# Two levels of a causal 4-token tree merged into one block, in the third branch of a hybrid decoder layer

## The chip, the cores and the metric

The kernel runs on one core of one Trainium2 chip. The metric is the device time of one launch in microseconds (us). Before the change it is 2781.73 us, the median of three runs (2780.98 to 2782.83).

## The reference

One decoder layer on 2048 tokens of width 1024, with 16 meta tokens in front. The normalised input goes through one projection, then through three causal mixers of four heads of 128, and gates and an output projection join them. The change touches only the third mixer, a gated linear recurrence (HGRN2). For one head, with queries `q`, keys `k`, values `v` and forget factors `f` per channel:

```
G = cumsum(log f) over the chunk
dec[i, j, d] = exp(G[i, d] - G[j, d])   for j <= i, else 0
a[i, j] = sum_d q[i, d] * k[j, d] * dec[i, j, d]
o = (q * exp(G)) @ state + a @ v
state = state * exp(G_end) + (k * exp(G_end - G))^T @ v
```

The entry `a[i, j]` between a key token j and a later token i needs the product of all factors `f` of the tokens j+1 to i, channel by channel, so it is no plain matrix product.

## The kernel before, in words

The sequence is worked through in four segments (`j`, 512 tokens each, `TQ`), and a segment in `NT` = 4 tiles of 128 tokens. Channels lie on the 128 partitions, tokens along the free dimension. `dense_work` (L1322) yields the projections and output products; each fp32 product is three matmuls with split operands (`mm3`, L167 to L169). At the bottom of the program every mixer's scan is woven into that stream by `weave` (L1392): each `yield` of a scan names an amount of time, and for it a share of dense matmuls is recorded. A scheduler of the tile framework then fixes each engine's order by its own estimate of times. The scans of heads 0 and 1 run side by side (`both`, L1284), then those of heads 2 and 3; so there are eight pairs, two in each segment.

`hg_scan` (L1103) computes `a` without exponentials of differences. It goes through seven levels, `s` = 1, 2, 4, ... 64. At level `s` the tokens are split into blocks of 2s; the pairs to be filled are those with j in the left and i in the right half. Two running tables are kept: `pf` holds, for a token, the product of the factors from the start of its block of `s` up to it, and `sf` the product from after it to the end of its block. The left halves of `kql` become `k * sf` (L1130; at level 1 a copy on GpSimd, L1128), the right halves `q * pf` (L1126). Then TensorE multiplies `kql` with itself, and only the entries of this level count. For s up to 16 that is sixteen 32x32 matmuls into one PSUM tile `z` (L1162), four tiles by four groups of 32 tokens; the text calls them one block. VectorE takes the level's entries out of `z` with a predicated copy (L1166) under the mask `lvl[:, lv]`, into the tile `AD`, which goes to the diagonal of `at` at level 16. For s = 32 and 64 the products at L1148 and L1136 fill `at` directly. L1178 and L1179 bring `sf` and `pf` to the next level; at level 1 two GpSimd instructions set `sf` (L1175, L1176). After the last level `at`, the values and the state `Sh` are multiplied (L1196 to L1199).

GpSimd also multiplies q by k for the diagonal (L1106), and `put_ob` (L398 to L402) has it subtract the high part of finished heads (`ob`, by the helper at L118). A sum over channels turns that product to tokens on TensorE (L380) and reduces it on VectorE (L367). The masks come from `c_lvl` through `load_levels` (L1465), once.

Of the kernel before, what the change touches and what calls it, by code (L numbers as in the profile page):

```python
# [15 lines left out]
P = 128  # L16
# [3 lines left out]
META = 16  # L20
TQ = 512
NQ = SEQ // TQ
NT = TQ // P
# [16 lines left out]
def kernel(  # L40
# [21 lines left out]
    nc = tc.nc  # L62
# [12 lines left out]
    def nm(s):  # L75
        uid[0] += 1
        return f"{s}_{uid[0]}"
# [5 lines left out]
    def slot(tag, shape=(P, WQ), dt=F32, bufs=None):  # L83
        return pool.tile(list(shape), dt, tag=tag, name=nm(tag), bufs=bufs or BUFS[tag])
# [10 lines left out]
    def p_z():  # L95
        return ps_z.tile([P, 512], F32, tag="z", name=nm("z"))
# [1006 lines left out]
    def hg_scan(j, h, st):  # L1103
        pf, kk, qq, vt, gate = st.pop(h)
# [4 lines left out]

        sf = slot("S")  # L1110
        at, ad = AT[h % 2], AD[h % 2]
        s = 1
        lv = 0
        while s < P:
            def v4(t):
                r_ = t[:, META:].rearrange("p (b two s) -> p b two s", two=2, s=s)
                return r_[:, :, 0], r_[:, :, 1]

            nb = TQ // (2 * s)
            kql = slot("S")  # L1120
            kl_, kr_ = v4(kql)
            pl_, pr_ = v4(pf)
            fl_, fr_ = v4(sf)
            kkl, _ = v4(kk)
            _, qqr = v4(qq)
            nc.vector.tensor_mul(kr_, qqr, pr_)  # L1126
            if s == 1:
                nc.gpsimd.tensor_copy(kl_, kkl)  # L1128
            else:
                nc.vector.tensor_mul(kl_, kkl, fl_)  # L1130
            z = p_z()
            if s == 64:

                for n in range(NT):
                    c, o = META + n * P, 64 * (n % 2)
                    nc.tensor.matmul(  # L1136
                        z[o : o + 64, n // 2 * 64 : n // 2 * 64 + 64], kql[:, c : c + 64], kql[:, c + 64 : c + P],
                        start=True, stop=True,
                    )
                for g in range(2):  # L1140
                    nc.scalar.copy(
                        at[:64, g::2, 64:], z[64 * g : 64 * g + 64, :P].rearrange("p (n c) -> p n c", n=2)
                    )
            elif s == 32:
                for n in range(NT):
                    for b in (0, 64):
                        c, o = META + n * P + b, b + 32 * (n % 2)
                        nc.tensor.matmul(  # L1148
                            z[o : o + 32, n // 2 * 32 : n // 2 * 32 + 32], kql[:, c : c + 32],
                            kql[:, c + 32 : c + 64], start=True, stop=True,  # L1150
                        )
                for b in (0, 64):
                    for g in range(2):
                        nc.scalar.copy(
                            at[b : b + 32, g::2, b + 32 : b + 64],
                            z[b + 32 * g : b + 32 * g + 32, :64].rearrange("p (n c) -> p n c", n=2),
                        )
            else:
                for n in range(NT):
                    for b in range(4):  # L1160
                        c = META + n * P + 32 * b
                        nc.tensor.matmul(  # L1162
                            z[32 * b : 32 * b + 32, n * 32 : (n + 1) * 32], kql[:, c : c + 32], kql[:, c : c + 32],
                            start=True, stop=True,
                        )
                nc.vector.copy_predicated(  # L1166
                    ad, lvl[:, lv : lv + 1].broadcast_to([P, NT, 32]),
                    z[:, :P].rearrange("p (n c) -> p n c", n=NT),
                )
                if s == 16:  # L1170
                    for b in range(4):
                        sl = slice(32 * b, 32 * b + 32)
                        nc.scalar.copy(at[sl, :, sl], ad[sl])
            if s == 1:
                nc.gpsimd.tensor_copy(fl_, pr_)  # L1175
                nc.gpsimd.memset(fr_, 1.0)  # L1176
            else:
                nc.vector.tensor_mul(fl_, fl_, pr_[:, :, s - 1 : s].broadcast_to([P, nb, s]))  # L1178
            nc.vector.tensor_mul(pr_, pr_, pl_[:, :, s - 1 : s].broadcast_to([P, nb, s]))  # L1179
            s *= 2  # L1180
            lv += 1
            yield 2.5
# [139 lines left out]
    def dense_work():  # L1322

        xs = norm_x0()
        for j in range(nq):
            y, yh, yl = [None] * KC, [None] * KC, [None] * KC
            pool_share[0] = 5
            for h in range(H):
                yield from sb_proj(j, xs, h, sst)
                if j == 0 and h == 0:  # L1330
                    load_levels()
# [76 lines left out]
    with tc.issue_after(marks["act"]), tc.issue_after(marks["dve"]), tc.issue_after(marks["pool"]):  # L1408
# [54 lines left out]
        lvl = const.tile([P, 5, 32], mybir.dt.uint8, name="lvl")  # L1463

        def load_levels():  # L1465
            lv32 = slot("D", (P, 5, 32))
            for b in range(4):
                sl = slice(32 * b, 32 * b + 32)
                nc.sync.dma_start(lv32[sl], c_lvl[sl, :5, sl])
            nc.vector.tensor_copy(lvl, lv32)  # L1470

    for j in range(nq):
# [104 lines left out]
```

## Time and profile before

| | |
|---|---|
| median of three runs | 2781.73 us |
| the profiled execution, its own time | 2781.62 us |
| its span, first to last instruction | 2779.8 us |
| TensorE busy | 2734.3 us, 98% |
| VectorE busy | 1469.8 us, 53% |
| ScalarE busy | 962.5 us, 35% |
| GpSimd busy | 744.0 us, 27% |
| mean granted TensorE clock | 0.997 |

The profiled execution lies 0.1 us below the median and 1.8 us above its span. Busy time of TensorE counts pipelined matmuls whose modelled ends overlap, so the price of a matmul is read from the starts in the timeline, not from its duration. A row of the timeline gives the start, the time, engine, line, operation and count; a note in brackets is the engine's idle time before it and what ended that.

### The profile page before, as it was taken

What the parts mean: (1) busy time and instruction counts of PE and PEld (TensorE: products, weight loads), DVE (VectorE), ACT (ScalarE), POOL (GpSimd) and SP (SyncE); (2) the same over time, 40 slices, a digit from 0 to 9 for tenths busy, and PEclk for the clock granted to TensorE, in tenths of its full rate; (3) what the DMA queues carried; (4) which work ended last, traced back from release to release, by engine and by line L of the source; (5) the groups of instructions that cost most, each with busy time, mean ns of one, the idle gap of its engine ahead of it and who ended that gap; (6) DMA issues with size and microseconds to landing.
All of it is one profiled execution on the core that took longest, in us unless ns stands there. A gap on an engine that the chain in (4) does not pass through costs nothing. (4 is left out here: it accounts for less than half of the span.)

```text
span 2779.8 us, 46064 instructions
## 1 busy us (share of the span) xinstructions
PE 2734.3 (98%) x17616; PEld 2258.6 (81%) x17616; DVE 1469.8 (53%) x2890; ACT 962.5 (35%) x2255; POOL 744.0 (27%) x1011
## 2 busy tenths in 40 slices
PE   7999999999999999999999999999999999999999
PEld 6898788888887888778888888877888877888887
DVE  5467637744357545543255775554325577556521
ACT  5454343343345212222144641222224455313120
POOL 4555214433132302112022240111212232302111
PEclk9999999999999999999999999999999999999999
DMA  7667746679554654547755456344764443554556
GB/s 259 227 205 255 264 164 217 237 255 322 188 169 148 194 175 129 159 152 245 231 176 175 145 168 189 115 151 148 250 209 148 157 160 121 170 157 122 160 159 211
DMA packets 200064, 520.51 MB, mean 187 GB/s; under 512 B 43104, under 2 KB 44064, under 8 KB 199844
## 3 DMA queue, kind: packets, MB, share of 16 engines
q1 hardware_dynamic: 199556, 517.50, 57.2%
q8 instruction: 139, 2.28, 0.3%
q14 instruction: 81, 0.66, 0.1%
q10 hardware_dynamic: 288, 0.07, 0.0%
HBM read 397.18 MB, written 120.31 MB: 186 GB/s over the span
## 5 line engine op out<-in xcount | busy, mean ns | idle before, releaser
L167 PE MATMUL acc<-xh,w 128*128 128x512 f32 (+2 forms) x2248 | 860.0, 383 | 4.5 <-DVE D L454 1.2
L168 PE MATMUL acc<-xl,w 128*128 128x512 f32 (+2 forms) x2248 | 847.3, 377 | 0.3 <-DVE xl L260 0.2
L169 PE MATMUL acc<-xh,w 128*128 128x512 f32 (+2 forms) x2248 | 845.1, 376 | 1.7 <-DVE w L118 1.7
L167 PEld LDWEIGHTS acc<-xh,w 128*128 128x128 f32 x2248 | 425.1, 189 | 80.4 <-DVE D L454 2.1
L169 PEld LDWEIGHTS acc<-xh,w 128*128 128x128 f32 x2248 | 425.1, 189 | 74.8 <-DVE w L118 2.2
L168 PEld LDWEIGHTS acc<-xl,w 128*128 128x128 f32 x2248 | 424.8, 189 | 69.7 <-DVE xl L260 1.3
L528 DVE TENSOR_TENSOR_SCAN S<-S,zero 128x128 f32<-128x128 f32 (+4 forms) x216 | 197.3, 917 | 143.1 <-ACT S L522 124.6
L118 POOL TENSOR_TENSOR w<-wraw,w 128x512 fp32r<-128x512 f32 x106 | 149.5, 1412 | 282.7 <-ACT w L147 246.9
L534 POOL TENSOR_TENSOR S<-S,S 128x256 f32<-128x256 f32 (+2 forms) x108 | 94.2, 873 | 396.4 <-DVE S L528 262.5
L522 ACT ACTIVATE S<-z,rq 128x128 f32<-128x128 f32 (+4 forms) x216 | 116.5, 539 | 132.4 <-PE z L169 85.2
L147 ACT CAST w<-wraw 128x512 fp32r<-128x512 f32 x182 | 112.3, 618 | 130.4 <-PE acc L169 59.2
L118 DVE TENSOR_TENSOR S<-tr,S 128x512 fp32r<-128x512 f32 (+4 forms) x176 | 104.9, 606 | 47.9 <-ACT S L562 47.4
L730 DVE SCALAR_TENSOR_TENSOR D<-D,cw,D 128x512 f32<-128x512 f32 (+1 forms) x144 | 120.2, 835 | 17.2 <-ACT D L728 15.0
L167 PE MATMUL acc<-ob,w 128*128 128x512 f32 x312 | 125.8, 405 | 1.4 <-ACT ob L401 1.4
L168 PE MATMUL acc<-ob,w 128*128 128x512 f32 x312 | 124.4, 399 | 0.0
L169 PE MATMUL acc<-ob,w 128*128 128x512 f32 x312 | 123.3, 396 | 0.0
L167 PE MATMUL av<-xh,w 128*128 128x512 f32 (+2 forms) x304 | 119.7, 394 | 0.7 <-ACT D L1059 0.7
L168 PE MATMUL av<-xl,w 128*128 128x512 f32 (+2 forms) x304 | 118.1, 389 | 0.0
L169 PE MATMUL av<-xh,w 128*128 128x512 f32 (+2 forms) x304 | 117.5, 386 | 0.0
L523 ACT ACTIVATE S<-z,rq 128x128 f32<-128x128 f32 (+4 forms) x216 | 116.0, 537 | 0.0
L562 ACT CAST S<-tr 128x512 fp32r<-128x512 f32 (+4 forms) x176 | 90.8, 529 | 64.4 <-PE tr L558 64.2
L1246 POOL TENSOR_TENSOR y<-y,g 128x512 f32<-128x512 f32 x32 | 46.8, 1461 | 236.3 <-DVE g L1244 236.3
(389 smaller groups left out, 4916.7 us busy)
## 6 DMA issues: line engine op xcount, KB each, us to landing
w<-wk SPq DMA_DIRECT2D x555, 512.0 KB, 3.5
wk<-w SPq DMA_DIRECT2D x184, 512.0 KB, 3.5
wraw<-in_w_in_dram SPq DMA_DIRECT2D x142, 256.0 KB, 3.8
D<-in_xq_dram SPq DMA_DIRECT2D x56, 256.0 KB, 4.3
S<-rows SPq DMA_DIRECT2D x48, 256.0 KB, 4.9
S<-dv SPq DMA_DIRECT2D x48, 256.0 KB, 4.3
out_dram<-D SPq DMA_DIRECT2D x32, 256.0 KB, 4.6
S<-dk SPq DMA_DIRECT2D x24, 264.0 KB, 3.0
```

Source lines behind the costliest of these rows:

```text
L118: (eng or nc.gpsimd).tensor_sub(out_, a, hi.bitcast(F32))
L147: nc.scalar.copy(hi, raw)
L167: nc.tensor.matmul(dst, lh, rh, start=first, stop=False)
L168: nc.tensor.matmul(dst, lh, rl, start=False, stop=False)
L169: nc.tensor.matmul(dst, ll, rh, start=False, stop=last)
L522: nc.scalar.activation(pc[:, :n], z[:, :n], AF.Sigmoid, scale=rq[:, NT + i : NT + i + 1])
L523: nc.scalar.activation(at[:, :n], z[:, :n], AF.Sigmoid, scale=rq[:, i : i + 1])
L528: nc.vector.tensor_tensor_scan(pc[:, 0:n][:, ::-1], pc[:, 0:n][:, ::-1], zero1.broadcast_to([P, n]), 1.0 if carry[i] is None else pc[:, n ...
L534: eng.tensor_mul(at[:, :n], at[:, :n], pc[:, 1 : n + 1])
L562: nc.scalar.copy(ath[:kw, cs_], tr[:kw, cs_])
L730: nc.vector.scalar_tensor_tensor(dst[:, c0:], raw[:, c0 + i : c0 + i + n], cw[:, ci, i : i + 1], dst[:, c0:], ALU.mult, ALU.add)
L1246: nc.gpsimd.tensor_add(y[e], y[e], g)
```

## The change

The levels s = 1 and s = 2 become one step on blocks of four tokens (0 to 3). Two tiles, `lh` and `rh`, take the place of `kql`: `lh` holds k0 f1, k1, k2 f3, k3, and `rh` holds, at the places 0 to 3, q3, q1, q2 f2, q3 f2 f3. One block of sixteen matmuls `lh` by `rh` then holds the entries of the pairs 0-1, 0-2, 1-2, 0-3 and 1-3 at their own places. The pair 2-3 needs another right side than the pairs 0-3 and 1-3; it stands in the column of token 0, which no pair uses, and a second predicated copy moves that column to the place of token 3. The mask of the first copy is level 2's with the level-1 column of token 1 joined to it, once, in `load_levels`. Two GpSimd copies fill the plain parts of `lh` and `rh`; four VectorE products fill the rest. After the copies `sf` and `pf` are brought to level 4 by four products, a GpSimd copy and a memset. The two yields of 2.5 become one of 5.0, and the loop starts at s = 4.

```diff
-        s = 1
-        lv = 0
+        def blocks(z, lh, rh):
+            for n in range(NT):
+                for b in range(4):
+                    c = META + n * P + 32 * b
+                    nc.tensor.matmul(
+                        z[32 * b : 32 * b + 32, n * 32 : (n + 1) * 32], lh[:, c : c + 32], rh[:, c : c + 32],
+                        start=True, stop=True,
+                    )
+            return z[:, :P].rearrange("p (n c) -> p n c", n=NT)
+        def quad(t):
+            return t[:, META:].rearrange("p (b i) -> p b i", i=4)
+        fq, kq, qq4, sq_ = quad(pf), quad(kk), quad(qq), quad(sf)
+        lh, rh = slot("S"), slot("S")
+        lq, rq = quad(lh), quad(rh)
+        mul = nc.vector.tensor_mul
+        nc.gpsimd.tensor_copy(lq[:, :, 1::2], kq[:, :, 1::2])
+        nc.gpsimd.tensor_copy(rq[:, :, 0:2], qq4[:, :, 1::2][:, :, ::-1])
+        mul(sq_[:, :, 1], fq[:, :, 2], fq[:, :, 3])
+        mul(lq[:, :, 0::2], kq[:, :, 0::2], fq[:, :, 1::2])
+        mul(rq[:, :, 2], qq4[:, :, 2], fq[:, :, 2])
+        mul(rq[:, :, 3], qq4[:, :, 3], sq_[:, :, 1])
+        zv = blocks(p_z(), lh, rh)
+        nc.vector.copy_predicated(ad, lvl[:, 1:2].broadcast_to([P, NT, 32]), zv)
+        nc.vector.copy_predicated(
+            ad[:, :, 3::4], lvl[:, 0:1, 3::4].broadcast_to([P, NT, 8]), zv[:, :, 0::4]
+        )
+        mul(sq_[:, :, 0], fq[:, :, 1], sq_[:, :, 1])
+        nc.gpsimd.tensor_copy(sq_[:, :, 2], fq[:, :, 3])
+        nc.gpsimd.memset(sq_[:, :, 3], 1.0)
+        mul(fq[:, :, 1], fq[:, :, 0], fq[:, :, 1])
+        mul(fq[:, :, 3], fq[:, :, 1], sq_[:, :, 1])
+        mul(fq[:, :, 2], fq[:, :, 1], fq[:, :, 2])
+        yield 5.0
+        s = 4
+        lv = 2
...
             nc.vector.tensor_mul(kr_, qqr, pr_)
-            if s == 1:
-                nc.gpsimd.tensor_copy(kl_, kkl)
-            else:
-                nc.vector.tensor_mul(kl_, kkl, fl_)
+            nc.vector.tensor_mul(kl_, kkl, fl_)
...
-            if s == 1:
-                nc.gpsimd.tensor_copy(fl_, pr_)
-                nc.gpsimd.memset(fr_, 1.0)
-            else:
-                nc.vector.tensor_mul(fl_, fl_, pr_[:, :, s - 1 : s].broadcast_to([P, nb, s]))
+            nc.vector.tensor_mul(fl_, fl_, pr_[:, :, s - 1 : s].broadcast_to([P, nb, s]))
...
+            nc.vector.tensor_copy(lv32[:, 1, 1::4], lv32[:, 0, 1::4])
             nc.vector.tensor_copy(lvl, lv32)
```

In the changed program the matmuls of all blocks stand at L1118, the two new predicated copies at L1140 and L1141, that of the later levels at L1198, the right and left products of the loop at L1167 and L1168, the tables' at L1203 and L1204, the level of 32 at L1186.

The scheduler sets the order anew, so rows move beyond the lines of the diff. On TensorE, the second pair of heads of the second segment, before (`acc` dense products, `tr` a turn to tokens, `z` a block):

```order
L380 MATMUL tr_12989<-ident,S_12986 128x128 x4
L1162 MATMUL z_12999<-S_12996 32x32 x16
L167 MATMUL acc_12976<-xh_7675,w_2535_12972 128x512
L168 MATMUL acc_12976<-xl_7676,w_2535_12972 128x512
L169 MATMUL acc_12976<-xh_7675,w_2535_12972 128x512
L167 MATMUL acc_12976<-xh_7723,w_2535_12972 128x512
L168 MATMUL acc_12976<-xl_7724,w_2535_12972 128x512
L169 MATMUL acc_12976<-xh_7723,w_2535_12972 128x512
L1162 MATMUL z_13029<-S_13026 32x32 x16
```

and now, from the same turn to tokens on:

```order
L380 MATMUL tr_12921<-ident,S_12918 128x128 x4
L1118 MATMUL z_12936<-S_12929,S_12928 32x32 x16
L167 MATMUL acc_12902<-xh_7860,w_2531_12900 128x512
L168 MATMUL acc_12902<-xl_7861,w_2531_12900 128x512
L169 MATMUL acc_12902<-xh_7860,w_2531_12900 128x512
L167 MATMUL acc_12902<-xh_7908,w_2531_12900 128x512
L168 MATMUL acc_12902<-xl_7909,w_2531_12900 128x512
L169 MATMUL acc_12902<-xh_7908,w_2531_12900 128x512
L167 MATMUL acc_12902<-xh_7956,w_2531_12900 128x512
L168 MATMUL acc_12902<-xl_7957,w_2531_12900 128x512
L169 MATMUL acc_12902<-xh_7956,w_2531_12900 128x512
L167 MATMUL acc_12971<-ob_11674,w_2516_12806 128x512
```

Blocks stood alone between dense matmuls, and still do; two of them are gone from the pair, and where the next one stood six dense matmuls later dense work goes on. TensorE's order, counted over all four segments, has 1024 block matmuls in 66 runs where it had 1280 in 77.

On VectorE, the start of the first pair of the third segment, before (`D_17769` and `D_18488` are the tables `pf` of the two heads):

```order
L398 TENSOR_TENSOR S_18461<-tr_18456,D_17713 128x512
L1126 TENSOR_TENSOR S_18635<-D_17828,D_17769 128x256
L1126 TENSOR_TENSOR S_18688<-D_18523,D_18488 128x256
L1179 TENSOR_TENSOR D_17769<-D_17769 128x256
L1126 TENSOR_TENSOR S_18721<-D_17828,D_17769 128x128x2
L1130 TENSOR_TENSOR S_18721<-D_17770,S_18634 128x128x2
```

and now (`D_17658` and `D_18377` are those tables):

```order
L398 TENSOR_TENSOR S_18350<-tr_18345,D_17602 128x512
L1136 TENSOR_TENSOR S_18524<-D_17659,D_17658 128x256
L1135 TENSOR_TENSOR S_18523<-D_17658 128x128
L1137 TENSOR_TENSOR S_18525<-D_17717,D_17658 128x128
L1136 TENSOR_TENSOR S_18595<-D_18378,D_18377 128x256
L1137 TENSOR_TENSOR S_18596<-D_18412,D_18377 128x128
L1135 TENSOR_TENSOR S_18594<-D_18377 128x128
L1138 TENSOR_TENSOR S_18525<-D_17717,S_18523 128x128
```

The first block of a pair hung on VectorE's first product; the first block of four hangs on the seventh (L1138 into `S_18525`).

On TensorE, later in the same pair, before (levels 8 and 16 of one head and 16 of the other, then level 32):

```order
L169 MATMUL acc_19069<-xh_14195,w_3719_19067 128x512
L167 MATMUL acc_19069<-xh_14233,w_3719_19067 128x512
L1162 MATMUL z_18888<-S_18885 32x32 x16
L1162 MATMUL z_18922<-S_18919 32x32 x16
L1162 MATMUL z_18957<-S_18954 32x32 x16
L1148 MATMUL z_18997<-S_18994 32x32 x8
L168 MATMUL acc_19069<-xl_14234,w_3719_19067 128x512
```

and now the same blocks:

```order
L169 MATMUL acc_18930<-xh_14008,w_3708_18926 128x512
L1118 MATMUL z_18749<-S_18746 32x32 x16
L1118 MATMUL z_18783<-S_18780 32x32 x16
L1118 MATMUL z_18818<-S_18815 32x32 x16
L167 MATMUL acc_18930<-xh_14046,w_3709_18928 128x512
L168 MATMUL acc_18930<-xl_14047,w_3709_18928 128x512
L169 MATMUL acc_18930<-xh_14046,w_3709_18928 128x512
L167 MATMUL acc_18930<-xh_14084,w_3709_18928 128x512
L1186 MATMUL z_18858<-S_18855 32x32 x8
```

The run of three blocks now stands earlier in the dense product, behind its fourth part of eight and not inside its seventh, and four dense matmuls have come between it and the matmuls of level 32. From the start of the pair to the run's third block there are 72 dense matmuls of 512 columns where there were 79. SP's order of DMAs is unchanged.

## Rows read from the trace of the kernel before

**Rows 1.** The page, busy time of the engines (us, share of span, instructions).

```profile
PE 2734.3 (98%) x17616; PEld 2258.6 (81%) x17616; DVE 1469.8 (53%) x2890; ACT 962.5 (35%) x2255; POOL 744.0 (27%) x1011
```

**Rows 2.** Waits of TensorE in the third branch: us in total, times, longest.

```profile
PE z L1148 <- DVE S L1126: 1.4, 2, 0.8
PE z L1162 <- DVE S L1126: 1.0, 1, 1.0
```

**Rows 3.** Groups by line, the blocks: busy us, mean ns of one, idle before.

```profile
L1162 PE MATMUL z<-S 128*32 128x32 f32 x2560 | 37.1, 199 | 1.0 <-DVE S L1126 1.0
```

**Rows 4.** Timeline of TensorE, one block alone: start us, us.

```profile
1103.90 0.39 PE L168 MATMUL acc<-xl,w 128*128 128x512 f32 x1
1104.13 0.40 PE L169 MATMUL acc<-xh,w 128*128 128x512 f32 x1
1104.46 0.46 PE L1162 MATMUL z<-S 128*32 128x32 f32 x32
1104.85 0.50 PE L168 MATMUL acc<-ob,w 128*128 128x512 f32 x1
1105.19 0.39 PE L169 MATMUL acc<-ob,w 128*128 128x512 f32 x1
```

**Rows 5.** Timeline of TensorE, a run of 6 records and one of 128.

```profile
437.88 0.40 PE L167 MATMUL acc<-ob,w 128*128 128x512 f32 x1
438.21 0.26 PE L1162 MATMUL z<-S 128*32 128x32 f32 x6
438.40 0.50 PE L168 MATMUL acc<-ob,w 128*128 128x512 f32 x1
438.74 0.39 PE L169 MATMUL acc<-ob,w 128*128 128x512 f32 x1
...
2539.70 0.40 PE L169 MATMUL av<-ob,w 128*128 128x512 f32 x1
2540.03 1.45 PE L1162 MATMUL z<-S 128*32 128x32 f32 x128
2541.41 0.50 PE L168 MATMUL acc<-ob,w 128*128 128x512 f32 x1
2541.74 0.39 PE L169 MATMUL acc<-ob,w 128*128 128x512 f32 x1
```

**Rows 6.** VectorE: one line's ns (min/median/max), and groups by form (busy us, mean ns).

```profile
L1126 DVE TENSOR_TENSOR S<-D,D x112: 408/420/1559, 427.9 to 2624.6; 128x256 f32<-128x256 f32 x112
...
L1166 DVE COPY_PREDICATED AD<-lvl,z 128x128 f32<-128x128 uint8 x80 | 23.5, 296 | 41.8 <-PE z L1162 41.8
L1003 DVE TENSOR_TENSOR r<-D,z 128x128 f32<-128x128 f32 x32 | 9.1, 284 | 17.9 <-PE z L1000 17.7
L534 DVE TENSOR_TENSOR S<-S,S 128x128 f32<-128x128 f32 x16 | 7.1, 443 | 1.9
```

**Rows 7.** Timeline of VectorE, first pair of the third segment.

```profile
1793.48 0.94 DVE L1126 TENSOR_TENSOR S<-D,D 128x256 f32<-128x256 f32 x2
1794.34 1.52 DVE L1179 TENSOR_TENSOR D<-D 128x256 f32<-128x256 f32 x1
...
1796.99 1.49 DVE L1178 TENSOR_TENSOR S<-S,D 128x256 f32<-128x256 f32 x1
1798.52 1.39 DVE L1179 TENSOR_TENSOR D<-D 128x256 f32<-128x256 f32 x1
...
1814.53 0.41 DVE L1130 TENSOR_TENSOR S<-D,S 128x256 f32<-128x256 f32 x1
1814.87 0.41 DVE L1179 TENSOR_TENSOR D<-D 128x256 f32<-128x256 f32 x1
```

**Rows 8.** Timeline of GpSimd, same pair.

```profile
1796.91 4.16 POOL L118 TENSOR_TENSOR ob<-S,ob 128x512 fp32r<-128x512 f32 x3
```

**Rows 9.** Timeline of TensorE, same pair.

```profile
1798.76 0.46 PE L1162 MATMUL z<-S 128*32 128x32 f32 x32
...
1815.76 0.46 PE L1162 MATMUL z<-S 128*32 128x32 f32 x32 [1.02 <-DVE S L1126]
1816.77 0.33 PE L1148 MATMUL z<-S 128*32 128x32 f32 x16 [0.55 <-DVE S L1126]
...
1817.42 0.63 PE L169 MATMUL acc<-xh,w 128*128 128x512 f32 x1
1817.84 0.63 PE L167 MATMUL acc<-xh,w 128*128 128x512 f32 x1
...
1820.79 0.39 PE L168 MATMUL av<-xl,w 128*128 128x512 f32 x1
```

**Rows 10.** One microsecond of that stretch: busy us by engine, granted clock, DMA share, GB/s.

```profile
1818.00:1819.00 1.00, 1.00 (x4) 0.81 (x3) 1.00 (x5) 0.01 (x1) 0.00 (x0) 0.50 0.00 0
```

**Rows 11.** Timeline of TensorE, a wait in the last segment's attention.

```profile
2307.00 0.50 PE L558 MATMUL tr<-ident,S 128*16 128x128 f32 x3 [1.41 <-POOL S L534]
```

**Rows 12.** Second pair of the third segment: an early product (VectorE) and the first block (TensorE).

```profile
1869.53 1.52 DVE L1126 TENSOR_TENSOR S<-D,D 128x256 f32<-128x256 f32 x1
...
1888.22 0.46 PE L1162 MATMUL z<-S 128*32 128x32 f32 x32
```

More of the change, by code (lines that the diff above doesn't have):

```diff
@@ L1158, in hg_scan @@
             else:
[L1159 to L1169, printed above, removed]
+                zv = blocks(z, kql, kql)
+                nc.vector.copy_predicated(ad, lvl[:, lv : lv + 1].broadcast_to([P, NT, 32]), zv)
                 if s == 16:
```

## The prediction

> **What bounds the kernel now.** I read the page's first part first. TensorE is busy 98% of the span and VectorE 53% [rows 1], so work taken off VectorE, ScalarE, GpSimd or the DMA queue buys nothing by itself; work taken off TensorE does, and so does a wait of TensorE. Second, TensorE's waits: they are few, and of those that belong to the third branch two are left, 1.0 us before a 32x32 block and 1.4 us in two pieces before the next level, all for VectorE's products at L1126 [rows 2]. Third, the group of L1162: the blocks of levels 1 to 16 are 2560 matmul records [rows 3]. They are 80 blocks (five levels, four heads, four segments), so 32 records each, two for each of the 16 matmuls in the source. Its 199 ns for one is a latency of pipelined work and no price. Fourth, therefore, the timeline of TensorE around such blocks, for the price.
>
> **The change part by part.**
>
> *TensorE.* Levels 1 and 2 of a head now need one block where they needed two, so 16 of 80 blocks go. A 128x512 matmul starts 0.23 us after the one before. From L169 at 1104.13 to L169 at 1105.19 there are 1.06 us; two steps of 0.23 are the dense matmuls' own, so the block between them costs 0.59 us [rows 4]. By the same count a run of 6 records costs 0.86 - 0.47 = 0.39 and a run of 128 costs 2.04 - 0.47 = 1.57 [rows 5]. So most of a lone block is the cost of breaking into the dense stream (about 0.36 us); records inside a run cost 8 to 10 ns. Between the 32-record and the 128-record run one block more costs (1.57 - 0.59) / 3 = 0.33 us. The ends for the 16 blocks are thus 16 x 0.33 = 5.3 us, all inside longer runs, and 16 x 0.59 = 9.4 us, all alone. The order decides. In six of the eight pairs of heads two breaks go with the two blocks: 1.18 us each, 7.1 together. In the first pair of the third segment six runs become five: 0.36 + 32 x 2 x 0.0085 = 0.9. In the first pair of the last segment the blocks are cut up more (five runs become seven) and nothing is left. Sum: **8.0 us less on TensorE**.
>
> *VectorE.* Per head six products of 256 elements per partition and two predicated copies of 0.296 us go; one product of 256, seven of 128, a predicated copy of 128 and one of 32 come. A free product of 256 takes 0.42 us [rows 6], and such products start 0.34 us apart when nothing is in the way [rows 7]. For a product of 128 with both inputs in SBUF the rows go from 0.443 us (L534, in a stage shared with GpSimd) to 0.284 (L1003, one input in PSUM) [rows 6]. I take the low end, since it fits the 256-wide row less half its elements; then they start 0.20 us apart. The 32-wide copy lies between nothing and 0.296; I take 0.1. By starts: before 6 x 0.34 + 2 x 0.20 = 2.4 us per head, now 0.34 + 7 x 0.20 + 0.20 + 0.1 = 2.0. With 0.443 for the seven it would be up to 1.1 us more per head than that. VectorE gains 0.4 us per head or loses 0.7; TensorE's dense work covers both outside the two places below. The one small copy at the start of L1495 is a single instruction far from any wait and costs nothing.
>
> *GpSimd.* Two copies of 256 stay two, and half a copy comes while the memset halves. GpSimd is at 27% [rows 1]. Its copies stand ahead of the same `ob` subtractions as before, so nothing new is queued behind them. SP's queue is unmoved; no DMA is added.
>
> *Where the cover is thin.* In the first pair of the third segment VectorE works without a gap and TensorE waits twice. Products that should take 0.42 take 1.52, 1.49 and 1.39 there [rows 7], each while GpSimd's two-input work runs (three `ob` subtractions last 4.16 us) [rows 8]. Those subtractions and products are the same six per pair after the change and each holds up one VectorE product, so I leave that loss as it is. The Trainium skill ("SBUF — State Buffer", section "SBUF: two separate sides") says that GpSimd and a VectorE instruction with two SBUF inputs take a shared port pair exclusively and that the loser waits for the whole instruction. The trace agrees, 1.49 us against 0.42. That rule speaks against the change, which raises the two-input products of the two levels from 6 to 8 per head: if the four extra ones of a pair met a GpSimd instruction each (1.07 us) in the two thin places, 8.6 us would be added and the time would be 2784.1; by the count of GpSimd's instructions nothing is.
>
> What does move is the meeting point of the two engines. TensorE waits 1.02 us before the third block of a run of three [rows 9]. VectorE's queue from the pair's first product up to that block's last input shrinks from 34 products of 256 to 24 of 256 and 14 of 128, and from seven predicated copies to five and two small ones. By starts that is 10 x 0.34 + 2 x 0.20 less, 14 x 0.20 + 2 x 0.1 more: VectorE comes 0.8 us sooner. TensorE's queue up to the same block holds two blocks less (0.9 us) and also 7 dense matmuls less (72 for 79, 1.6 us), because the order puts the run earlier in the dense product; TensorE comes 2.6 us sooner. The wait grows by 1.8, to 2.8 us. The 32-block behind it, which waited 0.55 more, now has four dense matmuls ahead of it and no wait. So this place goes from 1.57 to 2.8: **1.2 us given back**. In the last segment's first pair, at the block that waited 0.82 us [rows 2], TensorE comes 1.2 us sooner (5 dense matmuls less and next to nothing from the blocks), VectorE 0.5 sooner: **0.7 us given back**. At the first block of a pair TensorE comes 0.2 to 0.9 us later (one to four dense matmuls more stand ahead), but the block's last input is now VectorE's seventh product of the pair, not the first. The lead is 5.3 us in the third segment (product at 1793.48 [rows 7], block at 1798.76 [rows 9]); six products with three of them held up take 6 x 0.34 + 3 x 1.07 = 5.3. That just holds, so I count no wait.
>
> After the first of these waits the dense matmuls start 0.43 us apart in place of 0.23 (1817.42 to 1817.84) [rows 9] and the granted clock of that stretch is 0.50, the 1.2 GHz level [rows 10]. That is in the time of before, and I let it stand.
>
> Sum: 8.0 - 1.2 - 0.7 = 6.1 us. The profiled execution took 2781.62 us (its span 2779.8 and 1.8 around it), 0.1 below the median of 2781.73. 2781.6 - 6.1 gives 2775.5; **I forecast 2775.5 us**, 0.22% below the median. A measurement of this kernel tells about 0.2% (5.6 us) from no change, so the border of faster is 2776.2.
>
> **The rivals.**
>
> *The thin places get easier.* If the quad's shorter products and one level less let VectorE ahead of TensorE, the 2.4 us of waits [rows 2] go, and so does the slow stretch behind one of them: eight matmuls from 1817.42 to 1820.79 at 0.42 for 0.23, 1.6 us [rows 9]. 2781.6 - 8.0 - 4.0 = 2769.6. If the waits only stay as they are, 2773.6. For it: VectorE's queue is shorter. Against it: TensorE's shrinks more.
>
> *Blocks are cheaper than I take them.* At 0.33 us each, 5.3 us go; with the 1.9 given back, 2778.2. For it: in the third and last segment blocks do stand in runs. Against it: in six of eight pairs they stand alone in both orders.
>
> *A new wait at the block of four (the slow side).* It needs four VectorE products and two GpSimd copies where the first block needed one of each. The lead of 5.3 us is just filled as worked out above; one more product held up makes a wait of 1.07. A wait of 1.0 us with 1.6 us of slow clock behind it, in the four first pairs, is 10.4 us: 2781.6 - 6.1 + 10.4 = 2785.9, which is 0.15% more and still no change. It turns slower by over 0.2% (2787.3) once such a pair loses 2.9 us, that is from a wait of 1.3 us. Second pairs cannot do it: in the third segment their products start at least 18.7 us ahead of their first block [rows 12]. By the Trainium skill's rule above, this is where the extra held-up products would land.
>
> *Shifts elsewhere.* The scheduler also moves rows in the attention and gated-delta part of the last segment, where TensorE waits (1.41 us at 2307.00 [rows 11]). The rows right around that wait keep their order, so I put this at 1.5 us either way.
>
> **How the numbers follow.** Forecast case (blocks 8.0, given back 1 to 3 us): 0.50, its own range 2774 to 2777.5, of which somewhat over half lies below the border. Waits unchanged or gone (2769.6 to 2773.6): 0.25. Cheaper blocks: 0.09. A new wait at the block of four: 0.12, a third of it slower. Shifts elsewhere alone deciding: 0.04. Faster: 0.30 + 0.25 + 0.02 = 0.57; slower 0.04; same 0.39. The range reaches from the case with both waits gone, 2769.5, to about half of the new-wait case, 2780.5.
>
> **What would show it.** The blocks' records fall from 2560 to 2048. TensorE's busy time falls by about 8 us, and its waits for VectorE in the third branch rise from 2.4 us to about 4.3, still at two places, in the first pairs of the last two segments. A block alone still costs 0.59 us. Waits at the line of the new block of four (L1118), or waits spread over four pairs, would show the slow rival; no wait at all in the third branch would show the fast one. If the busy time falls by clearly less than 8 us, the price of a block was wrong.

## The result, and the profile after

The changed kernel takes 2790.47 us, the median of eight runs (2786.32 to 2793.83). The kernel before has a median of 2781.61 in eight runs of the same series (2779.71 to 2784.17). The ratio is 1.0032, with a 95% interval of 1.0023 to 1.0042: **slower by 0.32%, 8.9 us**, where 6.2 us less had been forecast. The profiled execution takes 2790.91 us; its span is 2789.1, 9.3 more than before. One run of the kernel before in a later series, at 2877.11 us in the chip's slow state, is left out of all comparisons.

The busy times, to be read beside [rows 1], and the blocks, beside [rows 3]:

```profile
PE 2732.0 (98%) x17104; PEld 2255.4 (81%) x17104; DVE 1483.5 (53%) x2923; ACT 963.9 (35%) x2255; POOL 740.8 (27%) x1027
```

```profile
L1118 PE MATMUL z<-S 128*32 128x32 f32 x1536 | 23.3, 201 | 10.4 <-DVE dcol L367 5.3 <-DVE AD L1141 2.5 <-DVE S L1167 2.4
...
L1118 PE MATMUL z<-S,S 128*32 128x32 f32 x512 | 8.4, 200 | 0.2 <-DVE S L1138 0.2
```

The 512 block matmuls that should go are gone (2048 for 2560). The idle time ahead of the blocks went from 1.0 us [rows 3] to 10.6. TensorE's waits in the third branch, which were 2.4 us [rows 2] (us in total, times, longest):

```profile
PE z L1118 <- DVE dcol L367: 5.3, 3, 2.6
...
PE av L169 <- DVE w L118: 2.7, 1, 2.7
...
PE z L1118 <- DVE AD L1141: 2.5, 1, 2.5
PE z L1118 <- DVE S L1167: 2.4, 2, 2.0
...
PE z L1118 <- DVE S L1138: 0.2, 1, 0.2
```

They sum to 13.1 us, and all lie in the first pairs of the four segments; the second pairs have none. Only the last row (0.2 us) is a wait for the quad's own operands. The first is for the reduction of q times k at L367: the block and that sum's turn to tokens share four PSUM buffers, and the next block may not be written until the reduction has read the old contents. The third is the same for the second predicated copy of a block of four, which reads the block's PSUM tile last. The second is the low part of a dense weight. None of these three is an operand of the block, though the copy at L1141 is one that the change adds. They all stand in VectorE's queue **behind** the quad's products. VectorE in the first pair of the third segment, to be read beside [rows 7]:

```profile
1800.24 0.60 DVE L1136 TENSOR_TENSOR S<-D,D 128x256 f32<-128x256 f32 x1
1800.77 0.60 DVE L1135 TENSOR_TENSOR S<-D 128x128 f32<-128x128 f32 x1
1801.28 1.51 DVE L1137 TENSOR_TENSOR S<-D,D 128x128 f32<-128x128 f32 x1
...
1804.32 1.49 DVE L1138 TENSOR_TENSOR S<-D,S 128x128 f32<-128x128 f32 x1
1805.73 1.50 DVE L1145 TENSOR_TENSOR S<-D,S 128x128 f32<-128x128 f32 x1
1807.14 1.49 DVE L1138 TENSOR_TENSOR S<-D,S 128x128 f32<-128x128 f32 x1
1808.55 0.38 DVE L1145 TENSOR_TENSOR S<-D,S 128x128 f32<-128x128 f32 x1
1808.84 0.67 DVE L1148 TENSOR_TENSOR D<-D 128x128 f32<-128x128 f32 x2
...
1811.34 0.68 DVE L367 TENSOR_REDUCE dcol<-tr 128x4 f32<-128x512 f32 x1
...
1812.60 0.30 DVE L1141 COPY_PREDICATED AD<-lvl,z 128x32 f32<-128x32 uint8 x1
...
1813.93 0.42 DVE L1167 TENSOR_TENSOR S<-D,D 128x256 f32<-128x256 f32 x1
```

Three things are to be seen. A short product, when nothing disturbs it, takes 0.38 us, and the next starts 0.29 later (1808.55 to 1808.84). Beside GpSimd's copies it takes 0.60. Four of the nine that start before 1808.55 take 1.5 us each, and GpSimd's rows say why:

```profile
1801.25 1.28 POOL L1106 TENSOR_TENSOR S<-D,D 128x512 f32<-128x512 f32 x1
1802.48 0.60 POOL L1133 COPY S<-D 128x256 f32<-128x256 f32 x1
...
1804.28 4.10 POOL L118 TENSOR_TENSOR ob<-S,ob 128x512 fp32r<-128x512 f32 x3
```

One product is held for the whole of L1106, three for the three subtractions at L118. So the reduction at L367 comes 11.10 us after the pair's first product. Before, it came 6.35 us after it, as VectorE's eighth instruction of the pair; the other row below is used further on:

```profile
1799.83 0.68 DVE L367 TENSOR_REDUCE dcol<-tr 128x4 f32<-128x512 f32 x1
...
1805.23 0.42 DVE L1126 TENSOR_TENSOR S<-D,D 128x256 f32<-128x256 f32 x1
```

TensorE pays there, and at 2549.65 in the last segment:

```profile
1812.08 0.46 PE L1118 MATMUL z<-S 128*32 128x32 f32 x32 [2.15 <-DVE dcol L367]
1814.49 0.34 PE L1118 MATMUL z<-S 128*32 128x32 f32 x8 [1.96 <-DVE S L1167]
...
2549.65 0.46 PE L1118 MATMUL z<-S 128*32 128x32 f32 x32 [2.54 <-DVE AD L1141]
...
2551.51 0.63 PE L168 MATMUL acc<-ob,w 128*128 128x512 f32 x1
2551.93 0.63 PE L169 MATMUL acc<-ob,w 128*128 128x512 f32 x1
```

The wait at 2549.65 ends with the second predicated copy of the second head. In VectorE's order it stands 1.54 us behind the first copy of the same tile, with four products between them, so the tile is held that much longer than by the first copy alone:

```profile
2547.68 0.29 DVE L1140 COPY_PREDICATED AD<-lvl,z 128x128 f32<-128x128 uint8 x1
...
2549.22 0.29 DVE L1141 COPY_PREDICATED AD<-lvl,z 128x32 f32<-128x32 uint8 x1
```

After the wait at 2549.65 the dense matmuls start 0.42 us apart in place of 0.23. The granted clock there, single microseconds after the pairs of the first, third and last segment (busy us by engine, granted clock, DMA share, GB/s):

```profile
446.00:447.00 1.00, 1.00 (x6) 0.50 0.97 268
1815.00:1816.00 1.00, 1.00 (x3) 0.50 0.06 16
2552.00:2553.00 1.00, 1.00 (x4) 0.50 0.00 0
```

It is the 1.2 GHz level, after TensorE had been idle for 2.7, 4.1 (two waits) and 2.5 us. Below, "lost to the clock" is one minus the granted clock, summed over all single microseconds of a trace. It was 8.5 us before and is 15.4 now.

**The balance of the 9.3 us:** 10.7 us of waits and 6.9 us of clock came, and what remains, about -8.3, is put down to the removed blocks, which run 1 tests.

Each run has its mean granted clock on record, to three digits, so the loss can be estimated for all of them: one minus that clock, times the span. It averages 16.4 us over the eight runs of the changed kernel and 9.3 over 61 of the kernel before (the series of runs 1 to 11). So some 7 of the 8.9 us are slow clock, and this is no accident of the two profiled executions.

### The profile page after: what moved, and what is told of

It is laid out like the page before. It is cut to its first block, busy times and chain, and to the rows that moved or that the text cites. A ratio compares the mean times of both kernels' runs of the same rounds, so it can differ in the third digit from the quotient of the medians.

```text
span 2789.1 us, 45076 instructions
## 1 busy us (share of the span) xinstructions
PE 2732.0 (98%) x17104; PEld 2255.4 (81%) x17104; DVE 1483.5 (53%) x2923; ACT 963.9 (35%) x2255; POOL 740.8 (27%) x1027
## 4 chain that ended last, share of the span: by engine, by line
PE 90%; DVE 6%; ACT 2%; POOL 1%; DMA 1%; issue 1%; SPq 0%; DVEq 0%; POOLq 0%; ACTq 0%
PE acc L167 21%; PE acc L168 20%; PE acc L169 20%; PE av L167 4%; PE av L168 4%; PE av L169 4%; PE tr L558 2%; PE acc L380 1%; PE z L167 1%; PE z L168 1%; PE z L169 1%; PE tr L380 1%; PE z L832 1%; DVE D L730 1%; PE z L1118 1%
## 5 line engine op out<-in xcount | busy, mean ns | idle before, releaser
L118 POOL TENSOR_TENSOR w<-wraw,w 128x512 fp32r<-128x512 f32 x106 | 142.6, 1346 | 285.4 <-ACT w L147 263.3
L118 DVE TENSOR_TENSOR S<-tr,S 128x512 fp32r<-128x512 f32 (+4 forms) x176 | 104.8, 605 | 48.2 <-ACT S L562 47.6
```

Source lines behind the costliest of these rows:

```text
L118: (eng or nc.gpsimd).tensor_sub(out_, a, hi.bitcast(F32))
```

## The experiments

Twelve runs followed. "Held up" below counts products of this branch that took more than 1.05 us, within 16 us of the first product of each of the four first pairs, instruction by instruction in the trace of VectorE. Before it was 15, in the changed kernel 18. The scheduler sets the order anew in every kernel, so rows beyond an edit move too; where they do not, the text says so.

**1. The blocks alone.** The kernel before; level 1 multiplies nothing, and both copies read level 2's block:

```
-            z = p_z()
-            if s == 64:
+            z = p_z() if s > 1 else None
+            if s == 1:
+                pass
+            elif s == 64:
...
+                for l_ in ((0, 1) if s == 2 else (lv,)):
+                    nc.vector.copy_predicated(ad, lvl[:, l_ : l_ + 1] ..., z ...)
```

> The kernel before, with the matmuls of level 1 left out: both predicated copies of levels 1 and 2 read level 2's block, so the entries of level 1 are wrong in value and everything on VectorE, ScalarE and GpSimd stays. Sixteen blocks go from TensorE and nothing else changes. Theory A (the TensorE term was right, the loss is made on VectorE): 8.0 us less, 2771 to 2776. Theory B (blocks are much cheaper than 0.59 us, so there was never much to win): 2777 to 2781. Theory C (the scheduler's new order elsewhere makes the loss): no statement, at most 1.5 us beside A.

2775.59 us, ratio to the kernel before 0.9975 (0.9965 to 0.9985). The profiled spans differ by 8.7 us, with the same loss to the clock (8.5 both). The waits rose a little, which fits TensorE arriving sooner:

```profile
PE z L1164 <- DVE S L1126: 2.6, 2, 1.6
...
PE z L1150 <- DVE S L1126: 1.1, 2, 0.5
```

That is 3.7 for 2.4 us. Theory A holds: the TensorE term was right, and B falls.

**2. The same block, by five wide products.** The changed kernel; the tables go through level 2's old forms, so seven short products become four wide ones:

```
-        mul(sq_[:, :, 1], fq[:, :, 2], fq[:, :, 3])
+        nc.gpsimd.tensor_copy(sq_[:, :, 0::2], fq[:, :, 1::2])
+        nc.gpsimd.memset(sq_[:, :, 1::2], 1.0)
         mul(lq[:, :, 0::2], kq[:, :, 0::2], fq[:, :, 1::2])
-        mul(rq[:, :, 2], qq4[:, :, 2], fq[:, :, 2])
-        mul(rq[:, :, 3], qq4[:, :, 3], sq_[:, :, 1])
+        mul(fq[:, :, 1::2], fq[:, :, 1::2], fq[:, :, 0::2])
+        mul(rq[:, :, 2:4], qq4[:, :, 2:4], fq[:, :, 2:4])
...
+        mul(sq_[:, :, 0:2], sq_[:, :, 0:2], fq[:, :, 3:4].broadcast_to([P, TQ // 4, 2]))
+        mul(fq[:, :, 2:4], fq[:, :, 2:4], fq[:, :, 1:2].broadcast_to([P, TQ // 4, 2]))
```

The last two lines replace everything after the predicated copies.

> The changed kernel, with the same single block of four, but its operands and tables made by five products of 256 elements in place of one of 256 and seven of 128; GpSimd gets one copy more and the memset doubles. Theory A (VectorE's many short products stand ahead of the reductions, predicated copies and weight parts that TensorE waits for): the waits of the first pairs fall from 13 us to 4 or less and the time to 2771 to 2778. Theory B (blocks cheap): 2778 to 2783. Theory D (GpSimd's copies for the block come late): a wait at the block itself, 2790 or more. Theory C (order elsewhere): 2786 to 2792, as the change.

2775.62 us, ratio 0.9975 (0.9965 to 0.9985): 14.9 us below the changed kernel, with the same single block. Held up: 11. Waits of the branch:

```profile
PE tr L380 <- DVE S L1208: 1.1, 1, 1.1
PE z L1171 <- DVE S L1164: 1.0, 1, 1.0
...
PE z L1118 <- issue: 0.6, 1, 0.6
...
PE z L1118 <- DVE AD L1142: 0.3, 1, 0.3
```

Theory A again. D falls: there are more GpSimd instructions ahead of the block, and no wait for them.

**3 and 4. GpSimd's subtraction as a copy, in the changed kernel and in the one before.**

```
-        sub_lo(ol, t[:, META:], oh)
+        nc.gpsimd.tensor_copy(ol, t[:, META:])
```

> The changed kernel, with GpSimd's subtraction that makes the low part of a finished head (two inputs) replaced by a copy (one input); the low part is left out of the output's value. Theory A1 (it is GpSimd's two-input work that holds up the short products): products held up to 1.5 us fall to four or fewer from the present number, the four first pairs lose 3 us less each, time 2776 to 2782. Theory A2 (number and place of the products alone put the others back): a gain of under 3 us, 2787 to 2791, waits at the same places.

> The kernel before with the same replacement of GpSimd's subtraction by a copy, for comparison with the changed kernel so treated. There the waits of the third branch are 2.4 us and the slow stretch behind one of them 1.6 us, so at most 4 us can go: 2777.5 to 2782. If it gains as much as the changed kernel does, the collisions are no part of the loss.

The changed kernel falls by 22 us to 2768.36, ratio 0.9951 (0.9936 to 0.9965). The kernel before falls by 5 us to 2777.51, ratio 0.9982 (0.9973 to 0.9991). The distance between the two is now -9.1 us, where it was +8.9. Held up: 7 and 5. VectorE in the third segment of the changed kernel so treated, with its one held-up product:

```profile
1789.29 0.53 DVE L1136 TENSOR_TENSOR S<-D,D 128x256 f32<-128x256 f32 x1
...
1792.06 1.52 DVE L1135 TENSOR_TENSOR S<-D 128x128 f32<-128x128 f32 x1
...
1797.71 0.68 DVE L367 TENSOR_REDUCE dcol<-tr 128x4 f32<-128x512 f32 x1
```

L367 stands behind the same products and comes after 8.42 us, not 11.10. The branch's waits for VectorE sum to 2.4 us, as before the change. A1 is right in kind; its gain was set too low, and its count of four or fewer held up does not hold. As the kernel before pays for its collisions too (5 us), they are no fault of the change alone; the change makes its time hang on them.

**5. The yield split.** A `yield 2.5` ahead of the table products, and 2.5 in place of the 5.0:

```
+        yield 2.5
         mul(sq_[:, :, 0], fq[:, :, 1], sq_[:, :, 1])
...
-        yield 5.0
+        yield 2.5
```

> The changed kernel with the yield of 5.0 in two of 2.5, one of them ahead of the tables' products; same instructions on every engine. In VectorE's order the first reduction that frees a PSUM buffer for a block then stands behind 14 products of the pair, not 19, in the three last segments. Theory P (place in VectorE's queue): it comes 2 to 3 us sooner, the waits for that reduction (5.3 us in sum) mostly go, 2781 to 2787. Theory H (only the holding up by GpSimd counts, wherever the products stand): the same GpSimd work stands beside the same products, 2788 to 2792.

2792.09 us, ratio 1.0034 (1.0023 to 1.0046): nothing gained. L367 came 1.3 us sooner in the third segment (9.78 for 11.10 us), less than expected, and no block waits for it any more. The waits stand elsewhere:

```profile
PE z L1118 <- DVE S L1168: 6.2, 3, 2.9
PE z L1187 <- DVE S L1168: 3.3, 2, 2.1
PE acc L167 <- DVE g L1270: 3.2, 1, 3.2
```

The first two are now operands of the next levels; the third is for a VectorE product that empties one of the dense accumulators. With 0.8 us at the block of four itself they sum to 13.5 us, where it was 13.1. Theory P falls; the time lies at the upper end of theory H's.

**6. The sum over channels taken after the last level.**

```
-        sum_cols(qk, dcol, 0, ps=p_tr)
...
+        sum_cols(qk, dcol, 0, ps=p_tr)
         qe = slot("S")
```

> The changed kernel with the sum over channels of q times k (the turn to tokens on TensorE and the reduction on VectorE) taken after the last level, so that no block waits for a buffer that this reduction frees; the number of products and of GpSimd's instructions stays. Theory P1 (the reduction behind the short products is the main harm): the waits for it are gone, 2779 to 2785. Theory P2 (any instruction behind the short products does the same harm, the predicated copies and weight parts too): TensorE reaches the next block sooner and waits there instead, 2786 to 2791.

2787.43 us, ratio 1.0022 (1.0013 to 1.0031). The reduction is out of the way, and other waits have its place:

```profile
PE z L1117 <- DVE S L1166: 4.4, 2, 2.4
...
PE av L169 <- DVE w L118: 3.1, 1, 3.1
PE z L1117 <- DVE AD L1140: 3.0, 1, 3.0
...
PE z L1117 <- DVE S L1137: 0.9, 1, 0.9
```

11.4 us in sum for 13.1. The copy at L1140 is here again the second one of a block of four. P2 is right: VectorE is late as a whole, and which of its instructions TensorE meets first is no matter. Runs 5 and 6 together reject my own first reading of the trace, that the place of L367 in the queue was the harm.

**7. The price of the products.** Behind the last output product of the kernel before, groups of products like these:

```
+    for r in range(2):
+        for o in (tc_, td):
+            nc.vector.tensor_mul(q4(o)[:, :, 2], q4(ta)[:, :, 2], q4(tb)[:, :, 2])
```

> The kernel before, with products added behind its last output product, when TensorE's work is nearly done: four each of 128 elements side by side, 128 elements 16 bytes apart, 256 in pairs (8 of every 16 bytes), 256 at every second place, 512; then four of the 16-byte kind beside GpSimd's copies of 256 and six beside its products of 512. If the price goes by elements: 0.28 us for both of 128 and 0.42 for 256. If it goes by the 16-byte step: 0.28 side by side, 0.38 for the step, 0.42 for 256. Beside copies 0.6; beside GpSimd's products one or two of the six are held up to 1.5 us and the others take 0.38. The time rises by some 10 to 20 us and says nothing.

The groups by line (duration in ns, min/median/max): L1500 side by side, L1503 at 16 bytes' distance, L1506 of 256, L1521 at 16 bytes' distance beside GpSimd's products.

```profile
L1500 DVE TENSOR_TENSOR S<-S,S x4: 278/280/633, 2730.9 to 2731.8; 128x128 f32<-128x128 f32 x4
...
L1503 DVE TENSOR_TENSOR S<-S,S x4: 373/378/383, 2732.0 to 2732.9; 128x128 f32<-128x128 f32 x4
...
L1506 DVE TENSOR_TENSOR S<-S,S x4: 407/408/408, 2733.2 to 2734.2; 128x256 f32<-128x256 f32 x4
...
L1521 DVE TENSOR_TENSOR S<-S,S x6: 384/394/1382, 2741.4 to 2745.5; 128x128 f32<-128x128 f32 x6
```

The distance decides: 0.378 us against 0.280 for the same number of elements, close to the 0.408 of twice as many. By starts it is 0.30 (1503's first at 2732.04, 1506's at 2733.24) against 0.335. The six beside two GpSimd products of 512 took 4.49 us together (2741.36 on). They all write one tile, as the four just before them do, and those start 0.43 us apart (2740.93 to 2741.36); six so spaced take 2.5 us. So 1.0 us is lost to each of GpSimd's two: two of the six took 1.38 and 1.37 us, the others 0.39. Beside copies nothing was learnt: GpSimd's two had all but ended (2738.66 and 1.09 us) when the four products began at 2739.65.

**8. Wide products, and the low part on VectorE.** Kernel 2, and

```
-        sub_lo(ol, t[:, META:], oh)
+        sub_lo(ol, t[:, META:], oh, nc.vector)
```

> The kernel of the five wide products, with the low part of the finished heads subtracted on VectorE in place of GpSimd (0.6 us each in place of 1.4; the same values). If holding up by GpSimd is what is left of the loss there: waits of the third branch near nothing, 2768 to 2774. If the subtractions, now in VectorE's own queue, put back what TensorE waits for: 2776 to 2784.

**2767.05 us**, ratio 0.9949 (0.9936 to 0.9963), the fastest of all, with nothing left out: 15.1 us below the kernel before in the same series (2782.18). Held up: 7. No block of the levels 1 to 16 waits, and 5.1 us are lost to the clock in its trace. Two short waits are left in the branch, of 0.6 us before a turn to tokens and 0.4 before a later level.

**9 and 10. The low part on VectorE, in the changed kernel and in the one before,** by the same line.

> The changed kernel as it is (seven short products), with the low part of finished heads subtracted on VectorE in place of GpSimd; values unchanged. If GpSimd's two-input work is what turns the change into a loss, this is as far below the next kernel (the one before, so treated) as TensorE's term says, 8 to 9 us, and comes to 2767 to 2773. If the number of short products is what matters, it gains little on the change: 2780 to 2788.

> The kernel before with the low part of finished heads on VectorE. From the run with a copy in its place (2777.5): 2774 to 2780. If moving the subtraction is worth much by itself, also without the merged block, 2770 or less, and then the gain of the merged block is smaller than 8 us there.

2771.69 us, ratio 0.9968 (0.9957 to 0.9979), and 2779.91, ratio 0.9998 (0.9989 to 1.0007). Moving the subtraction does nothing for the kernel before. For the changed one, products unaltered, it is worth 18.8 us, and the merged block then gains 8.2. The waits of the branch there fall from 13.1 to 3.5 us, and the loss to the clock, averaged over all runs, from 16.4 to 8.7. The 18.8 is the worth of the move together with the order that the scheduler then sets.

**11. The wide kernel with three idle products a head.**

```
+        for i_ in (1, 2, 3):
+            mul(quad(xt_)[:, :, i_], qq4[:, :, i_], kq[:, :, i_])
```

> The kernel of the five wide products with three short products per head added that nobody reads (q times k at every fourth place, into a tile of their own): VectorE's products for the block are then eight a head as in the changed kernel, while TensorE, the tables and GpSimd stay as in the wide one. Theory A (VectorE's work at the head of the first pairs is the loss): 2 x 3 x 0.29 us and one or two more held up, 3 to 4 us a pair, so the waits come back in the four first pairs: 2780 to 2789. Theory C (the wide kernel gained by another order or by its table chain, and the number of products is not what matters): 2774 to 2778.

2782.18 us, ratio 1.0006 (0.9997 to 1.0015): 6.6 us more than kernel 2, with nothing changed on TensorE or GpSimd. The two programs have the same instructions there in the same order, and VectorE's order differs by the inserted products alone; so no new order can be the cause. Held up: 18 for 11. The longest new wait, for the second predicated copy of a block, in the last segment:

```profile
2550.24 0.63 PE L1118 MATMUL z<-S 128*32 128x32 f32 x32 [2.83 <-DVE AD L1142]
```

Theory A holds, at its lower half.

**12. The changed kernel again,** unaltered.

> The changed kernel once more, for a second profiled execution. What belongs to the change returns at its places: TensorE's waits of 2 to 3 us in the first pairs and a stretch of granted clock 0.50 behind those at about 445, 1814 and 2551 us. If the stretches at 220 and 336 us, where the order is that of the kernel before, are a matter of the single execution, one or both are missing or others stand in their place; if they return, the change would have to act on them in a way not yet seen. Time 2786 to 2794.

2791.01 us. The waits are those of the first profile to 0.1 us, and the stretches of clock 0.50 behind them returned. The stretches at 220 and 336 us came back too. But they do not belong to the change. Run 7 is the kernel before, instruction by instruction, up to its last output product. TensorE at 218 us and the clock after it, in the kernel before and then in run 7:

```profile
218.38 0.66 PE L380 MATMUL acc<-ident,D 128*128 128x128 f32 x4 [2.20 <-ACT D L725]
...
221.00:222.00 1.00, 1.00 (x10) 1.00 0.13 53
```

```profile
219.60 0.66 PE L380 MATMUL acc<-ident,D 128*128 128x128 f32 x4 [2.20 <-ACT D L725]
...
221.00:222.00 1.00, 1.00 (x7) 0.50 0.02 8
```

The same wait of 2.20 us in the same program is followed by full clock in one execution and by 0.50 in the other. Nine of the ten profiles with this wait have the stretch; the one of the kernel before is the exception. The stretch at 336 us is in run 4 too, which has no merged block, and not in run 5, which up to there is the changed kernel. In the third segment it is the other way round: the waits of [rows 9] are 1.00 and 0.55 us in run 7, and the dense matmuls behind them start 0.23 us apart (1819.48 to 1819.71), without the slow clock of [rows 10]. What decides it in one execution stays open.

## Why the prediction was wrong

**TensorE's 8.0 us: right.** Taking the loss to the clock out of the spans, kernel 1 stands 8.7 us below the kernel before, 3 stands 8.3 below 4, and 9 stands 8.0 below 10. With the loss to the clock averaged over all runs of these kernels, the same distances are 8.0, 6.4 and 7.3, each with 1.1 to 1.3 us more of waits in the branch set against it. The fall of TensorE's busy time (2.3 us) was a poor test of it, since half clock lengthens the busy time.

**VectorE's step: wrong, and the forecast hung on it.** It said that "VectorE comes 0.8 us sooner" to the meeting point. At the right operand of the second head's next level, VectorE in the third segment came 11.75 us after the pair's first product before (at 1805.23), and 13.69 now (1813.93): 1.9 later. In the second segment it went from 13.40 us to 15.05, 1.7 later. At the instruction that the step counted to, the same operand of level 16, it went from 21.72 us (at 1815.20) to 24.16 (1824.40): 2.4 later. Two terms make the difference of about 2.5:

- *The short product.* It was taken at 0.284 us, starts 0.20 apart, from a row whose elements lie side by side. At 16 bytes' distance it is 0.378 and 0.30 (run 7). For 14 of them in a pair that is 1.4 us. The choice of the low end against 0.443 had no row of the same layout behind it.
- *The products held up.* "each holds up one VectorE product, so I leave that loss as it is" was the step that set the rule of the Trainium skill aside ("SBUF — State Buffer", section "SBUF: two separate sides"). GpSimd's two-input instructions are indeed the same six per pair, but before they did not each meet one: in the four first pairs they held up 4, 4, 3 and 3 products, and now 5, 5, 4 and 4 (one of the 15 above met another GpSimd instruction). A queue with more two-input products close together leaves fewer GpSimd instructions that fall on something else: in the third segment before, the last of the three subtractions ran beside the reduction at 1799.83, which reads PSUM and took its usual 0.68 us. One more in a pair is 1.1 us.

With 1.4 and 1.1 the step's -0.8 becomes +1.7, close to what the two segments show. Runs 3, 9 and 11 show both terms at work: without the subtractions on GpSimd the same short products do no harm, and three more of them without any other change bring 6.6 us back.

**The count of places: wrong.** The step looked for a wait at the quad's first block and at two later blocks, by their operands. At the first block it was right (0.2 us). At the two later blocks no wait is left (in the third segment the run of three starts at 1825.17 without one), since TensorE had already lost 4.1 us at earlier instructions of that pair. What TensorE met was whatever stood behind the products on VectorE: the reduction and the copies that free PSUM buffers, and a weight part in the first segment. So the first pairs of all four segments waited, 10.7 us more, where 1.9 us had been counted at two. Runs 5 and 6 show that the particular instruction is interchangeable.

**The slow clock: not counted.** The forecast let the stretches stand as they were. Behind the waits of the first, third and last segment there are now four of them (two in a row in the third) with 1.7 us lost in each, where there was one; the wait of 2.6 us in the second segment had none. Averaged over all runs, the four kernels with many waits (the changed one, 5, 6 and 11) lose 14 to 16 us to the clock, and kernels 1 to 4 and 8 to 10 lose 8 to 11, like the kernel before with 9.3. A single trace says less: that of kernel 2 lost 13.7 us, its nine runs 11.4 on average.

**The rivals.** The slow rival (a new wait in the four first pairs, with slow clock behind it) was the right kind, with the right four places; it was put at the block's operands, was given 1.0 us of wait where about 2.7 came, and a chance of 0.12. The case of four more products held up in each of the two thin places (2784.1) was right in kind as well: it was one more, in each of four. "Blocks are cheaper" and "shifts elsewhere" are out as causes, by run 1 and by runs 9 and 10.

The 6.9 us of clock between the two profiles are made up thus: the stretches behind changed waits (at 446, 1815 and 2552 us) lose 6.8 where [rows 10] belongs to one of 1.7, so 5.1 more; those at 220 and 336 us make 5.1 more; two that the kernel before had in the last segment and the first profile after has not make 3.4 less. The last two items, 1.7 us together, lie where the order did not change or where no run here separates causes, and runs 5 and 7 show that such a stretch can come or stay away in the same program: luck of the single executions is enough for them. The stretches behind the changed waits stood in both profiles of the changed kernel, and the 7 us by which the average over all runs rose fit them better than luck; that this rise comes from them alone is not shown.

## What to carry to other kernels

An engine at 53% can be the bound for ten microseconds at a time: where it works without a gap, count its queue up to every instruction that another engine needs, buffer releases and unrelated operands among them, not only up to the operands that the change makes. Saving TensorE's matmuls is worth their price only if the engine that feeds them does not get a longer queue for it; here the same merged block lost 8.9 us with seven short products beside GpSimd's work, and gained 6.9 with four wide ones in their place. And where two engines hold each other up, moving one's instructions to the other can be worth more than the change itself: 18.8 us for one word here (with the order that the scheduler then set), and nothing in the kernel before. A single trace of each kernel is not enough for the slow clock: the same program had a stretch of it in one execution and none in the other.

## What the runs showed of the hardware that was not expected

- A VectorE product of 128 elements 16 bytes apart costs 0.378 us, near the 0.408 of 256 elements; side by side it costs 0.280 (run 7).
- A predicated copy of 32 elements takes as long as one of 128 (0.30 and 0.29 us), but the next instruction starts 0.10 us after it, not 0.20 (1812.60 to 1812.70 in the third segment).
- Beside VectorE's two-input products, GpSimd's copies mostly take 0.57 to 0.62 us, for 128 elements as for 256, and with none beside them 0.40 to 0.43 (L1133, L1134 and L1146 of the changed kernel). VectorE's short products take 0.60 beside such copies in place of 0.38: both engines pay.
- The same wait of TensorE, 2.20 us at 218 us, is followed by half clock in run 7 and by full clock in the kernel before, which is the same program up to there.
